# Time mixing with receptance and gate in plain fp32, and another order around the merges

## The chip, the cores and the metric

The kernel runs on one core of one Trainium2 chip. The metric is the device time of one execution in microseconds (us); of several executions the median counts. The engines are TensorE (PE in the profile, its weight loads PEld), VectorE (DVE), ScalarE (ACT), GpSimd (POOL) and SyncE (SP, whose queue issues the weight loads from HBM). A matmul writes one of eight PSUM banks of 128 x 512 fp32; everything else lies in SBUF.

## The reference, cut to what matters

Eight layers run one after the other on 256 tokens of width 1024. Only the first, a time mixing layer of the RWKV-7 kind, is touched:

```python
rkv = einsum('nbtd,nde->nbte', xs[:3], w_rkv)         # receptance r, key k, value v
w_log = -softplus(-(w0 + tanh(xw @ w1) @ w2)) - 0.5
a = sigmoid(a0 + (xa @ a1) @ a2)
g = sigmoid(xg @ g1) @ g2                             # gate, 160 -> 1024
# per head, token by token:
S = S * w + (S a) b^T + v k^T ;  y = S r
out = ((groupnorm(y) * lnx_w + lnx_b + sum(r * k * r_k) * v) * g) @ w_o
```

The last sum, `sum(r * k * r_k)`, is called the bonus below.

## The kernel before, in words

**Products.** The inputs are fp32. Large weights come in units of 128 x 1024 through a `Feeder`: a load from HBM fills one of four raw buffers (`s_slot_79` to `s_slot_82`), ACT writes a rounded copy `hi` in the fp32r format (line 88) and DVE the rest `lo = raw - hi` (line 89) into one of four cut buffers, and the raw buffer is loaded again. A product is then three fp32r matmuls (`mm3`, lines 290 to 292). The plan of units is k, v, r of `a_w_rkv` (8 units each), then `a_w_o` (8 units). A matmul on plain fp32 operands needs no split, and the trace shows each as two instructions.

**The recurrence** is solved in two blocks b of 128 tokens and two halves H of eight heads. `rwkv_keys` turns keys (PE transposes, line 1702 for those in pairs, 1716 for others); `rwkv_strict` makes the masked scores SM (PE line 1848, DVE line 1850). `rwkv_base` inverts 16 x 16 triangles for all heads on DVE: first line 1747, 14 rounds of lines 1768 and 1769, last line 1774. `rwkv_merge` doubles the inverted blocks twice: PE 1791, DVE copy 1792, PE 1798, DVE 1800 and 1804, PE 1811, DVE copies 1818, PE 1824, DVE copies 1827. `rwkv_solve` makes further scores SN (1848), multiplies them with V (1863), and then goes to and fro: ACT copy 1876, PE 1879, DVE copy 1880, PE 1874. `rwkv_query` scales and turns the queries (DVE 1934, PE 1702) and makes the bonus: POOL 1937, DVE 1938 and 1940, POOL 1943 to 1947. `rwkv_gate` multiplies the gate, split by `gate_parts` (ACT 1911 and 1913, POOL 1912, DVE 1907, 1910, 1914), on lines 290 to 292 and 1925. Then the output product with `a_w_o` begins, again on lines 290 to 292, and the next layer (`ffn0`, lines 532 and 534).

**Order.** Functions are generators that `weave` steps in turn, and a scheduler then fixes, when the kernel is built, one order of instructions for each engine and each queue from their dependences, the numbers given to `pri`, and its own notion of durations. On the chip each engine keeps its order: an instruction that waits holds all behind it, on the SP queue as well. PSUM banks are handed out in rings (`rings(acc, tp, long, po)`). In the listings `bank_67` to `bank_74` are the banks 0 to 7.

Of the kernel before, what the change touches and what calls it, by code (L numbers as in the profile page):

```python
# [29 lines left out]
class Feeder:  # L30
# [38 lines left out]
    def prime(self):  # L69
        k = self.k  # L70
        while self.n_dma < len(self.plan) and self.raw_free:
            shape, pieces = self.plan[self.n_dma]
            t = self.raw_free.pop(0)
            v = self.view(t, shape)
            for c0, c1, src in pieces:
                k.nc.sync.dma_start(v[:, :, c0:c1], src)
            self.raw[self.n_dma] = (t, v)
            self.n_dma += 1

    def _split(self):  # L80
        k, i = self.k, self.n_split
        self.prime()
        t, raw = self.raw.pop(i)
        cut = self.cut_free.pop(0)
# [8 lines left out]
        self.prime()  # L93

    def get(self):
# [53 lines left out]
class K:  # L149
# [148 lines left out]
    def gemm_b_steps(self, nkt, widths, lhs, done, rk=2, tail=0, head=0, before_b1=None):  # L298

        W = self.W  # L300
        for h, width in enumerate(widths):
# [3 lines left out]
            def mms(b, chunk, kt0, n):  # L305
                hi, lo, _ = chunk
                for i in range(n):
                    kt = kt0 + i
                    lh, ll = lhs(kt, b)
                    self.mm3(ps[b], lh, ll, hi[:, i, :], lo[:, i, :], kt == 0, kt == nkt - 1)  # L310
# [1060 lines left out]
    def plan_rwkv(self):  # L1371
        out = []
        for n in (1, 2, 0):
            out += plan_b(self.a["a_w_rkv"][0, n], D, D)
# [40 lines left out]
    def rwkv(self):  # L1415
# [151 lines left out]
        while len(self.bg) > 1:  # L1567
            self.tick()
        W.lo_pool = False
        gate = self.gate_parts(hid)  # L1570
        self.weave([self.pri(1000, self.rwkv_merge(E[H])) for H in range(2)] + [self.pri(400, self.rwkv_gate(H, E[H], *gate)) for H in range(0)], n=2)
        solve = ([self.pri(400, self.rwkv_solve(H, 0, E[H], raw["v"][H])) for H in range(2)]
                 + [self.pri(400, self.rwkv_gate(H, E[H], *gate)) for H in range(0, 2)])
        if 0:
            self.rings(2, 4, 2)
            self.weave(solve, n=0)
            solve = []
        self.drain()
        W.lo_pool = False
# [115 lines left out]
    def feat_pairs(self, src, out, zeroed=()):  # L1695

        nc = self.nc
        for b in range(2):
# [84 lines left out]
    def rwkv_merge(self, E):  # L1783
# [3 lines left out]
        p1 = self.tp()  # L1787
# [6 lines left out]
        pz = self.tp()  # L1794
# [11 lines left out]
        p1 = self.tp()  # L1806
# [13 lines left out]
        pz = self.tp()  # L1820
# [33 lines left out]

    def rwkv_solve(self, H, b, E, V):
# [3 lines left out]
        SN = yield from self.rwkv_scores(E, b, E["A2"][b], 1, 0)  # L1859
        pr = self.bank("long")  # L1860
        cols = [slice(hd * 64, hd * 64 + 64) for hd in range(8)]
        for hd, c in enumerate(cols):
            nc.tensor.matmul(pr[:, c], SN[:, hd], V[:, b, c], start=hd == 0, stop=False, skip_group_check=True)
# [33 lines left out]
    def gate_parts(self, hid):  # L1897

        nc, A = self.nc, self.a
        raw = [self.slot([128, D]) for _ in range(2)]  # L1900
        nc.sync.dma_start(raw[0], A["a_g2"][0, :128])
        for i in range(3):
            nc.sync.dma_start(raw[1][32 * i:32 * i + 32], A["a_g2"][0, 128:])
        gh, gl, gs = (self.slot([128, D], F32R) for _ in range(3))
        h = self.slot([128, 4, T], F32R)
        nc.scalar.activation(h[:, 0], hid[:, 2], AF.Copy)
        nc.vector.tensor_tensor(h[:, 1], hid[:, 2], h[:, 0], op=OP.subtract)
        for i in range(2):
            nc.scalar.activation(h[32 * i:32 * i + 32, 2], hid[:32, 3], AF.Copy)
        nc.vector.tensor_tensor(h[64:96, 2], hid[:32, 3], h[:32, 2], op=OP.subtract)  # L1910
        nc.scalar.activation(gh, raw[0], AF.Copy)
        nc.gpsimd.tensor_tensor(gl, raw[0], gh, op=OP.subtract)
        nc.scalar.activation(gs[:96], raw[1][:96], AF.Copy)
        nc.vector.tensor_tensor(gs[32:64], raw[1][32:64], gs[32:64], op=OP.subtract)
        return h, gh, gl, gs

    def rwkv_gate(self, H, E, h, gh, gl, gs):
# [11 lines left out]
    def rwkv_query(self, H, E, raw, vecs):  # L1929
# [4 lines left out]
        nc.vector.tensor_tensor(EP, R, EP, op=OP.mult)  # L1934
        E["R2"] = []
        yield from self.feat_pairs(EP, E["R2"])
# [134 lines left out]
```

## Time and profile before

| what | value |
|---|---|
| median of three executions | 1428.81 us (1420.3 to 1430.14) |
| the profiled execution | 1423.76 us, its span 1421.9 us |
| PE busy over the span | 1339.9 us (94%) |
| DVE, ACT, POOL busy | 982.4, 723.2, 312.1 us |
| layer of the change | from the start to some 300 us, where the next layer's matmuls are under way |

The span is the traced part of the profiled execution, 1.9 us less than its time. All times in the rows below count from the start of the span. Busy shares are means over eight layers with different limits; the part of the trace that the change touches lies between 60 and 300 us.

### The profile page before, as it was taken

The page shows a single profiled execution, that of the slowest core. Times are in us where ns is not written, and L with a number is a line of the kernel's source. Part 1 is how long each engine was busy: PE and PEld are TensorE (multiplying, and loading weights), DVE is VectorE, ACT ScalarE, POOL GpSimd, SP SyncE. Part 2 cuts the span into 40 slices and gives each one's busy share as a digit, 9 for nine tenths or more (in the row PEclk, how much of TensorE's full clock was granted, in tenths as well). Part 3 has the DMA queues.
Part 4 walks back from the last instruction along what each step waited for, and adds up shares of the span by engine and source line. Part 5 has one row for each costly group of instructions (what it writes and reads, how often), then busy time and mean ns, then how long its engine had stood idle before and what let it go on. Part 6 is the DMA issues. An engine that isn't in the chain of part 4 may idle for free. (4 is left out here: it accounts for less than half of the span.)

```text
span 1421.9 us, 20925 instructions
## 1 busy us (share of the span) xinstructions
PE 1339.9 (94%) x7819; PEld 1116.4 (79%) x7819; DVE 982.4 (69%) x1712; ACT 723.2 (51%) x1276; POOL 312.1 (22%) x278
## 2 busy tenths in 40 slices
PE   7998799989999799999999999999999998999998
PEld 5786699778888687788877777788888776788887
DVE  7889545788854675678864688677633897687642
ACT  5843212566643575576654555555543545465431
POOL 4201621100000100133222353222322631111110
PEclk9998599999999899999999999999999999999999
DMA  8345002466672452275574544265763632266662
GB/s 259 120 128 181 2 16 80 159 204 183 193 237 89 147 169 60 90 217 183 178 225 150 178 148 119 87 202 185 227 194 96 206 114 80 74 195 191 191 197 87
DMA packets 153574, 214.79 MB, mean 151 GB/s; under 512 B 11700, under 2 KB 95900, under 8 KB 153472
## 3 DMA queue, kind: packets, MB, share of 16 engines
q1 hardware_dynamic: 152608, 210.31, 47.6%
q10 hardware_dynamic: 864, 3.15, 0.6%
q8 instruction: 61, 1.00, 0.3%
q14 instruction: 41, 0.34, 0.1%
HBM read 212.37 MB, written 1.05 MB: 150 GB/s over the span
## 5 line engine op out<-in xcount | busy, mean ns | idle before, releaser
L88 ACT ACTIVATE s_slot<-s_slot 128x1024 fp32r<-128x1024 f32 (+2 forms) x221 | 229.6, 1045 | 166.8 <-PE bank L292 104.6
L89 DVE TENSOR_TENSOR s_slot<-s_slot,s_slot 128x1024 fp32r<-128x1024 f32 (+1 forms) x180 | 224.7, 1254 | 102.7 <-ACT s_slot L88 102.1
L89 DVE TENSOR_TENSOR rwkv_slot<-s_slot,rwkv_slot 128x1024 fp32r<-128x1024 f32 (+4 forms) x121 | 151.8, 1261 | 91.7 <-ACT rwkv_slot L88 91.2
L88 ACT ACTIVATE rwkv_slot<-s_slot 128x1024 fp32r<-128x1024 f32 (+3 forms) x141 | 144.7, 1034 | 88.3 <-PE bank L292 52.3
L89 POOL TENSOR_TENSOR s_slot<-s_slot,s_slot 128x1024 fp32r<-128x1024 f32 x41 | 100.9, 2460 | 303.0 <-ACT s_slot L88 283.0
L532 PE MATMUL bank<-ffn_slot,s_slot 128*128 128x512 f32 x320 | 115.2, 401 | 5.4 <-DVE ffn_slot L537 5.4
L532 PE MATMUL bank<-ffn_slot,rwkv_slot 128*128 128x512 f32 x280 | 98.4, 395 | 0.0
L532 PE MATMUL bank<-mlp_slot,s_slot 128*128 128x512 f32 x272 | 96.7, 396 | 0.6 <-DVE mlp_slot L537 0.6
L266 POOL TENSOR_TENSOR rwkv_sm<-rwkv_sm,mhalf 128x1 f32<-128x1 f32 x32 | 19.8, 618 | 340.0 <-DVE rwkv_sm L263 339.2
L534 PE MATMUL bank<-ffn_slot,s_slot 128*128 128x256 f32 x320 | 89.9, 281 | 0.0
L534 PE MATMUL bank<-ffn_slot,rwkv_slot 128*128 128x256 f32 x280 | 77.8, 278 | 0.0
L532 PEld LDWEIGHTS bank<-ffn_slot,s_slot 128*128 128x128 f32 x320 | 61.2, 191 | 20.8 <-DVE ffn_slot L537 6.4
L534 PE MATMUL bank<-mlp_slot,s_slot 128*128 128x256 f32 x272 | 75.8, 279 | 0.0
L89 POOL TENSOR_TENSOR rwkv_slot<-s_slot,rwkv_slot 128x1024 fp32r<-128x1024 f32 (+1 forms) x20 | 47.3, 2364 | 92.6 <-ACT rwkv_slot L88 75.1
L290 PE MATMUL bank<-s_slot,mlp_slot 128*128 128x512 f32 x160 | 62.6, 391 | 0.1
L292 PE MATMUL bank<-s_slot,mlp_slot 128*128 128x512 f32 x160 | 62.3, 390 | 0.0
L291 PE MATMUL bank<-s_slot,mlp_slot 128*128 128x512 f32 x160 | 62.3, 389 | 0.0
L532 PEld LDWEIGHTS bank<-ffn_slot,rwkv_slot 128*128 128x128 f32 x280 | 52.5, 188 | 12.4 <-DVE ffn_slot L537 0.3
L534 PEld LDWEIGHTS bank<-ffn_slot,s_slot 128*128 128x128 f32 x320 | 61.3, 192 | 0.0
L532 PEld LDWEIGHTS bank<-mlp_slot,s_slot 128*128 128x128 f32 x272 | 51.0, 188 | 12.8 <-DVE mlp_slot L537 0.9
L534 PEld LDWEIGHTS bank<-ffn_slot,rwkv_slot 128*128 128x128 f32 x280 | 52.6, 188 | 0.2
L532 PE MATMUL bank<-mlp_slot,rwkv_slot 128*128 128x512 f32 x144 | 51.7, 398 | 0.6 <-DVE mlp_slot L537 0.6
(514 smaller groups left out, 3549.4 us busy)
## 6 DMA issues: line engine op xcount, KB each, us to landing
s_slot<-in_mlp_w_dram SPq DMA_DIRECT2D x128, 512.0 KB, 4.4
s_slot<-in_ffn_w_in_dram SPq DMA_DIRECT2D x88, 512.0 KB, 4.2
s_slot<-in_ffn_w_out_dram SPq DMA_DIRECT2D x44, 512.0 KB, 4.2
s_slot<-in_a_w_rkv_dram SPq DMA_DIRECT2D x24, 512.0 KB, 4.4
s_slot<-in_diff_w_in_dram SPq DMA_DIRECT2D x32, 256.0 KB, 4.2
s_slot<-in_dsa_w_in_dram SPq DMA_DIRECT2D x16, 512.0 KB, 4.1
s_slot<-in_a_w_o_dram SPq DMA_DIRECT2D x8, 512.0 KB, 3.9
s_slot<-in_o_w_dram SPq DMA_DIRECT2D x8, 512.0 KB, 3.9
```

The costliest lines, as they stand in the source:

```text
L88: k.nc.scalar.activation(hi, raw, AF.Copy)
L89: (k.nc.gpsimd if low else k.nc.vector).tensor_tensor(lo, raw, hi, op=OP.subtract)
L266: nc.gpsimd.tensor_tensor(r, u, self.mhalf[:, 0:1], op=OP.pow)
L290: mm(out, lh, rh, start=start, stop=False)
L291: mm(out, lh, rl, start=False, stop=False)
L292: mm(out, ll, rh, start=False, stop=stop)
L532: mm(o, wh[:, kt % 4, c], a.rearrange("p c t -> p (c t)"), start=kt == 0, stop=False, skip_group_check=True)
L534: mm(o[:, :T], wl[:, kt % 4, c], a[:, 0], start=False, stop=kt == 7, skip_group_check=True)
```

## The change

Receptance units are marked whole in the plan: they are not split, `mm3` makes one plain fp32 matmul of them (line 307 of the changed kernel) from the unsplit token mix, and the raw buffer is given back when the matmuls have used it. The gate is one pair of plain fp32 matmuls (1943, 1944) on unsplit weights. `rwkv_solve_in` (scores SN of block 0 and their product with V) and the turn of the queries of block 0 are woven with the merges, the merges take their banks from a ring of their own, and the rest of `rwkv_query` is now `rwkv_bonus`, written behind the merges, with the loads of its vectors.

```diff
@@ Feeder._split
         t, raw = self.raw.pop(i)
+        if self.whole(i):
+            self.parts[i] = (raw, None, t)
+            self.n_split += 1
+            return
@@ Feeder.put
-        self._give(unit[2])
+        if unit[1] is None:
+            self.raw_free.append(unit[2])
+            self.prime()
+        else:
+            self._give(unit[2])
@@ Feeder.advance
-        while not self.hold and self.n_split < min(self.cap, len(self.plan)) and self.cut_free:
+        while not self.hold and self.n_split < min(self.cap, len(self.plan)) and (
+                self.cut_free or self.whole(self.n_split)):
+            self.prime()
+            if self.n_split not in self.raw:
+                return
             self._split()
@@ mm3
+        if rl is None:
+            mm(out, lh, rh, start=start, stop=stop)
+            return
@@ rwkv
-        xr = shifted(0, True)
-        self.bg.append(project("r", xr))
+        xr = shifted(0)
+        self.bg.append(project("r", (xr, xr)))
...
-        gate = self.gate_parts(hid)
-        self.weave([self.pri(1000, self.rwkv_merge(E[H])) for H in range(2)] + [...], n=2)
-        solve = ([self.pri(400, self.rwkv_solve(H, 0, E[H], raw["v"][H])) for H in range(2)]
-                 + [self.pri(400, self.rwkv_gate(H, E[H], *gate)) for H in range(0, 2)])
+        gate = self.gate_weights()
+        self.bg += [self.rwkv_gate(H, E[H], hid, gate) for H in range(2)]
         self.drain()
         W.cap = W.n_split
-        self.rings(0, 4, 4)
+        self.rings(0, 4, 2)
+        self.ring["merge"] = self.banks[6:]
+        self.weave([self.pri(1000, self.rwkv_merge(E[H])) for H in range(2)]
+                   + halves(400, self.rwkv_solve_in, raw) + halves(0, self.rwkv_query, raw, 0))
+        self.ring["long"] += self.ring["merge"]
         vecs = [...]
-        self.weave(solve + [self.pri(400, self.rwkv_query(H, E[H], raw, vecs)) for H in range(2)])
+        self.weave([self.pri(400, self.rwkv_solve(H, 0, E[H], raw["v"][H])) for H in range(2)]
+                   + [self.pri(0, self.rwkv_reads(E[H], 0)) for H in range(2)] + halves(0, self.rwkv_query, raw, 1)
+                   + halves(0, self.rwkv_bonus, raw, vecs))
@@ rwkv_gate
-            self.mm3(p, h[:, 0, t], h[:, 1, t], gh[:, cols], gl[:, cols], True, False)
-            nc.tensor.matmul(p, h[:96, 2, t], gs[:96, cols], start=False, stop=True)
+            nc.tensor.matmul(p, hid[:, 2, t], w[0][:, cols], start=True, stop=False)
+            nc.tensor.matmul(p, hid[:32, 3, t], w[1][:32, cols], start=False, stop=True)
```

What the scheduler makes of it shows in its orders. In the changed kernel the lines move on: 89 becomes 93, 290 to 292 become 309 to 311, 1702 is 1719, 1791 is 1808, 1792 is 1809, 1798 is 1815, 1850 is 1867, 1879 is 1911, 1880 is 1912, 1934 is 1950, 1937 is 1959, 1938 is 1960, 1940 is 1962.

VectorE before, from the end of the base (1774) to the first copies of the merges (1792):

```order
L1774 STREAM_TRANSPOSE rwkv_slot_796<-rwkv_slot_794 128x512
L1799 TENSOR_SCALAR rwkv_slot_1070<-rwkv_slot_796,even_odd 128x16x16 x2
L1850 TENSOR_TENSOR rwkv_slot_1508<-bank_67,rwkv_slot_97 128x512
L1938 TENSOR_TENSOR rwkv_slot_612<-rwkv_slot_503,rwkv_slot_612 128x1024
L1940 TENSOR_REDUCE rwkv_sm_496<-rwkv_slot_612 128x16
L1938 TENSOR_TENSOR rwkv_slot_613<-rwkv_slot_511,rwkv_slot_613 128x1024
L1850 TENSOR_TENSOR rwkv_slot_1512<-bank_68,rwkv_slot_97 128x512
L1792 COPY rwkv_slot_792<-bank_72 128x16x16
```

VectorE now, the same stretch (1791 is the end of the base, 1809 the first copy):

```order
L1791 STREAM_TRANSPOSE rwkv_slot_776<-rwkv_slot_774 128x512
L93 TENSOR_TENSOR s_slot_86<-s_slot_79,s_slot_85 128x1024
L1950 TENSOR_TENSOR rwkv_slot_511<-rwkv_slot_605,rwkv_slot_511 128x1024
L93 TENSOR_TENSOR s_slot_88<-s_slot_79,s_slot_87 128x1024
L1867 TENSOR_TENSOR rwkv_slot_1131<-bank_67,rwkv_slot_97 128x512
L1867 TENSOR_TENSOR rwkv_slot_1135<-bank_68,rwkv_slot_97 128x512
L1816 TENSOR_SCALAR rwkv_slot_982<-rwkv_slot_776,even_odd 128x16x16 x2
L93 TENSOR_TENSOR s_slot_90<-s_slot_79,s_slot_89 128x1024
L1722 COPY rwkv_slot_1140<-bank_69 64x4x128
L1722 COPY rwkv_slot_1150<-bank_70 64x4x128
L1960 TENSOR_TENSOR rwkv_slot_604<-rwkv_slot_503,rwkv_slot_604 128x1024
L1962 TENSOR_REDUCE rwkv_sm_496<-rwkv_slot_604 128x16
```

Behind these stand 1960 for the other half and then 1809: the bonus's instructions still stand ahead of the first merge copy, and three splits of `a_w_o` units (line 93), all from the raw buffer 79, and four evacuations came in ahead of it.

The SP queue before, from the first `a_w_o` unit on:

```order
L76 DMA s_slot_79<-in_a_w_o_dram 128x2x512
L76 DMA s_slot_80<-in_a_w_o_dram 128x2x512
L76 DMA s_slot_81<-in_a_w_o_dram 128x2x512
L76 DMA s_slot_82<-in_a_w_o_dram 128x2x512
L76 DMA s_slot_79<-in_a_w_o_dram 128x2x512
L76 DMA s_slot_80<-in_a_w_o_dram 128x2x512
L1901 DMA rwkv_slot_1071<-in_a_g_dram 128x1024
L1903 DMA rwkv_slot_1072<-in_a_g_dram 32x1024 x2
```

The SP queue now, from the same place (`in_a_g_dram` is the gate's weight, 248 the helper that loads a vector into all partitions):

```order
L76 DMA s_slot_79<-in_a_w_o_dram 128x2x512
L76 DMA s_slot_80<-in_a_w_o_dram 128x2x512
L76 DMA s_slot_79<-in_a_w_o_dram 128x2x512
L76 DMA s_slot_81<-in_a_w_o_dram 128x2x512
L1932 DMA rwkv_slot_983<-in_a_g_dram 128x1024
L1933 DMA rwkv_slot_984<-in_a_g_dram 32x1024
L76 DMA s_slot_79<-in_a_w_o_dram 128x2x512
L76 DMA s_slot_82<-in_a_w_o_dram 128x2x512
L76 DMA s_slot_79<-in_a_w_o_dram 128x2x512
L248 DMA rwkv_slot_1463<-in_a_r_k_dram 128x1024
```

The first four `a_w_o` units that are split now all pass through raw buffer 79, one after the other, since the other three are held by receptance units; the load of `a_r_k`, which the bonus needs, waits in the built program for the last gate matmul (1944), whose weight buffer it takes over.

TensorE now, from the end of the receptance (307) to the first merge matmuls (1808); before, lines 1848, 290 to 292 and 1925 of half 0 alone stood here:

```order
L307 MATMUL bank_68<-s_slot_82,rwkv_slot_595 128x512 x2
L1719 MATMUL bank_69<-ident,rwkv_slot_503 128x128 x4
L1865 MATMUL bank_67<-rwkv_slot_215,rwkv_slot_623 128x256 x2
L1865 MATMUL bank_68<-rwkv_slot_227,rwkv_slot_636 128x256 x2
L1943 MATMUL bank_72<-rwkv_slot_983,rwkv_slot_207 128x512
L1943 MATMUL bank_73<-rwkv_slot_983,rwkv_slot_207 128x512
L1943 MATMUL bank_74<-rwkv_slot_983,rwkv_slot_207 128x512
L1943 MATMUL bank_71<-rwkv_slot_983,rwkv_slot_207 128x512
L1944 MATMUL bank_72<-rwkv_slot_984,rwkv_slot_207 128x512
L1944 MATMUL bank_73<-rwkv_slot_984,rwkv_slot_207 128x512
L1944 MATMUL bank_74<-rwkv_slot_984,rwkv_slot_207 128x512
L1944 MATMUL bank_71<-rwkv_slot_984,rwkv_slot_207 128x512
```

All four gate products now stand ahead of the merges, and two scores of SN (1865) read banks that held the receptance.

## Rows read from the trace of the kernel before

**Rows 1.** Busy time by stretch: length, then PE, PEld, DVE, ACT, POOL; clock, DMA.

```profile
91.50:126.80 35.30, 34.37 (x282) 28.62 (x281) 29.69 (x53) 13.64 (x19) 1.56 (x3) 1.00 0.45 144
126.80:139.80 13.00, 6.14 (x17) 3.18 (x15) 12.29 (x20) 4.09 (x6) 2.35 (x1) 0.68 0.87 281
139.80:152.10 12.30, 5.95 (x264) 5.15 (x264) 10.48 (x12) 0.00 (x0) 8.42 (x5) 0.50 0.01 3
152.10:163.70 11.60, 7.74 (x385) 7.31 (x384) 4.06 (x7) 5.59 (x10) 11.17 (x8) 0.50 0.02 4
163.70:175.90 12.20, 12.12 (x150) 9.62 (x151) 7.06 (x11) 1.58 (x4) 3.39 (x7) 0.50 0.01 1
175.90:182.20 6.30, 6.30 (x47) 5.64 (x45) 1.50 (x3) 3.11 (x6) 4.83 (x3) 1.00 0.01 3
182.20:239.10 56.90, 56.82 (x521) 53.55 (x520) 28.30 (x54) 7.35 (x14) 9.39 (x31) 1.00 0.08 29
```

**Rows 2.** PE in order of time around the receptance: start, length, line, operands, count.

```profile
95.71 0.59 PE L290 MATMUL bank<-s_slot,rwkv_slot 128*128 128x512 f32 x1
...
124.06 0.39 PE L290 MATMUL bank<-s_slot,rwkv_slot 128*128 128x512 f32 x1
...
126.55 0.39 PE L292 MATMUL bank<-s_slot,rwkv_slot 128*128 128x512 f32 x1
126.78 2.28 PE L1848 MATMUL bank<-rwkv_slot,rwkv_slot 128*128 128x256 f32 x8
```

**Rows 3.** PE in order of time, plain fp32 matmuls at the full clock.

```profile
58.91 1.98 PE L1639 MATMUL bank<-rwkv_slot,rwkv_slot 128*128 128x512 f32 x4
60.82 1.91 PE L1526 MATMUL bank<-rwkv_slot,rwkv_slot 128*32 128x256 f32 x8
...
207.63 3.67 PE L1848 MATMUL bank<-rwkv_slot,rwkv_slot 128*128 128x256 f32 x16
211.13 0.78 PE L1963 MATMUL bank<-rwkv_slot,rwkv_slot 128*128 128x64 f32 x6
```

**Rows 4.** DVE groups from 105.4 to 141.1 us: count, busy, mean ns.

```profile
L89 DVE TENSOR_TENSOR s_slot<-s_slot,s_slot 128x1024 fp32r<-128x1024 f32 x7 | 8.5, 1218 | 0.3 <-ACT s_slot L88 0.2
```

**Rows 5.** DVE in order of time: base, bonus, first merge copies.

```profile
105.42 0.68 DVE L1747 TENSOR_TENSOR rwkv_slot<-bank,tri 128x512 f32<-128x512 f32 x1
...
131.41 2.10 DVE L1768 TENSOR_TENSOR rwkv_slot<-rwkv_slot 128x288 f32<-128x288 f32 x1
...
134.03 1.22 DVE L1914 TENSOR_TENSOR rwkv_slot<-rwkv_slot,rwkv_slot 32x1024 fp32r<-32x1024 f32 x1
...
140.32 0.71 DVE L1774 STREAM_TRANSPOSE rwkv_slot<-rwkv_slot 128x512 f32<-128x512 f32 x1
...
144.74 3.35 DVE L1938 TENSOR_TENSOR rwkv_slot<-rwkv_slot,rwkv_slot 128x1024 f32<-128x1024 f32 x1 [1.71 <-POOL rwkv_slot L1937]
148.12 1.22 DVE L1940 TENSOR_REDUCE rwkv_sm<-rwkv_slot 128x16 f32<-128x1024 f32 x1
...
150.99 0.75 DVE L1792 COPY rwkv_slot<-bank 128x256 f32<-128x256 f32 x2
```

**Rows 6.** Loads issued between 100 and 136 us: count, size, median us to landing.

```profile
s_slot<-in_a_w_o_dram SPq DMA_DIRECT2D x8, 512.0 KB, 3.9
...
rwkv_slot<-in_a_lnx_w_dram SPq DMA_DIRECT2D x1, 512.0 KB, 6.3
```

**Rows 7.** ACT and POOL in order of time: a split's first half, the bonus's products.

```profile
127.78 1.05 ACT L88 ACTIVATE s_slot<-s_slot 128x1024 fp32r<-128x1024 f32 x1
...
142.36 4.64 POOL L1937 TENSOR_TENSOR rwkv_slot<-rwkv_slot,rwkv_slot 128x1024 f32<-128x1024 f32 x2
```

**Rows 8.** PE in order of time: merges and the start of the solve.

```profile
139.85 2.85 PE L1791 MATMUL bank<-rwkv_slot,rwkv_slot 32*32 32x16 f32 x194 [3.34 <-DVE rwkv_slot L1772]
...
152.18 2.77 PE L1798 MATMUL bank<-rwkv_slot,rwkv_slot 32*32 32x16 f32 x186
156.07 1.25 PE L1798 MATMUL bank<-rwkv_slot,rwkv_slot 32*32 32x16 f32 x70 [1.13 <-issue]
159.14 3.65 PE L1811 MATMUL bank<-rwkv_slot,rwkv_slot 32*32 32x32 f32 x128 [1.82 <-DVE rwkv_slot L1804]
163.78 2.08 PE L1848 MATMUL bank<-rwkv_slot,rwkv_slot 128*128 128x256 f32 x4 [0.99 <-ACT rwkv_slot L1926]
...
182.23 2.07 PE L1879 MATMUL bank<-rwkv_slot,rwkv_slot 64*64 64x64 f32 x32
```

**Rows 9.** PE in order of time: where the output product waits.

```profile
252.11 0.50 PE L290 MATMUL bank<-s_slot,rwkv_slot 128*128 128x512 f32 x1 [0.89 <-ACT rwkv_slot L280]
```

More of the change, by code (lines that the diff above doesn't have):

```diff
@@ L93, in _split, with whole @@
         self.prime()
+    def whole(self, i):
+        return len(self.plan[i]) > 2
     def get(self):
@@ L1373, in plan_rwkv @@
         for n in (1, 2, 0):
-            out += plan_b(self.a["a_w_rkv"][0, n], D, D)
+            units = plan_b(self.a["a_w_rkv"][0, n], D, D)
+            out += units if n else [(*u, True) for u in units]
         return out + self.plan_out(self.a["a_w_o"][0], 4)
@@ L1693, in pair_tile, with feat_pairs @@
         return t
-    def feat_pairs(self, src, out, zeroed=()):
+    def feat_pairs(self, src, out, zeroed=(), bs=range(2)):
         nc = self.nc
-        for b in range(2):
+        for b in bs:
             t = zeroed.pop(0) if zeroed else self.pair_tile()
@@ L1786, in rwkv_merge @@
         Moff, P1z, Xv, Yc, Y32, Y64 = (E[n] for n in ("Moff", "P1z", "Xv", "Yc", "Y32", "Y64"))
-        p1 = self.tp()
+        p1 = self.bank("merge")
         for h in range(16):
@@ L1793, in rwkv_merge @@
         yield
-        pz = self.tp()
+        pz = self.bank("merge")
         for h in range(16):
@@ L1805, in rwkv_merge @@
         yield
-        p1 = self.tp()
+        p1 = self.bank("merge")
         for h in range(16):
@@ L1819, in rwkv_merge @@
         yield
-        pz = self.tp()
+        pz = self.bank("merge")
         for h in range(16):
@@ L1853, in rwkv_scores, with rwkv_known, rwkv_solve_in @@
         return S
+    def rwkv_known(self, E, b, V):
+        pr = self.bank("long")
+        for hd in range(8):
+            c = slice(hd * 64, hd * 64 + 64)
+            self.nc.tensor.matmul(pr[:, c], E["SN", b][:, hd], V[:, b, c], start=hd == 0, stop=False,
+                                  skip_group_check=True)
+        return pr
+    def rwkv_solve_in(self, H, E, raw):
+        E["SN", 0] = yield from self.rwkv_scores(E, 0, E["A2"][0], 1, 0)
+        E["pr"] = self.rwkv_known(E, 0, raw["v"][H])
+        yield
     def rwkv_solve(self, H, b, E, V):
@@ L1858, in rwkv_solve @@
         SM, Y = E["SM", b], E["Y64"]
-        SN = yield from self.rwkv_scores(E, b, E["A2"][b], 1, 0)
-        pr = self.bank("long")
         cols = [slice(hd * 64, hd * 64 + 64) for hd in range(8)]
-        for hd, c in enumerate(cols):
-            nc.tensor.matmul(pr[:, c], SN[:, hd], V[:, b, c], start=hd == 0, stop=False, skip_group_check=True)
+        if b:
+            E["SN", b] = yield from self.rwkv_scores(E, b, E["A2"][b], 1, 0)
+            pr = self.rwkv_known(E, b, V)
+        else:
+            pr = E["pr"]
         if b:
@@ L1895, in rwkv_solve, with gate_weights, rwkv_gate @@
                                         op=OP.mult)
-    def gate_parts(self, hid):
+    def gate_weights(self):
         nc, A = self.nc, self.a
[L1900 to L1917, printed above, removed]
+        w = [self.slot([128, D]) for _ in range(2)]
+        nc.sync.dma_start(w[0], A["a_g2"][0, :128])
+        nc.sync.dma_start(w[1][:32], A["a_g2"][0, 128:])
+        return w
+    def rwkv_gate(self, H, E, hid, w):
         nc = self.nc
@@ L1923, in rwkv_gate, with rwkv_query, rwkv_bonus @@
             t = slice(b * 128, (b + 1) * 128)
-            self.mm3(p, h[:, 0, t], h[:, 1, t], gh[:, cols], gl[:, cols], True, False)
-            nc.tensor.matmul(p, h[:96, 2, t], gs[:96, cols], start=False, stop=True)
+            nc.tensor.matmul(p, hid[:, 2, t], w[0][:, cols], start=True, stop=False)
+            nc.tensor.matmul(p, hid[:32, 3, t], w[1][:32, cols], start=False, stop=True)
             nc.scalar.activation(G[:, b], p, AF.Copy)
             yield
-    def rwkv_query(self, H, E, raw, vecs):
+    def rwkv_query(self, H, E, raw, b):
+        if b == 0:
+            self.nc.vector.tensor_tensor(E["EP"], raw["r"][H], E["EP"], op=OP.mult)
+            E["R2"] = []
+        yield from self.feat_pairs(E["EP"], E["R2"], (), (b,))
+    def rwkv_bonus(self, H, E, raw, vecs):
         nc = self.nc
```

17 lines of the change are left out of this document (3 added, 14 removed).

## Prediction

> **What bounds the kernel now.** I read the table of the span by slices first, then busy time by stretch in the layer of the change. There TensorE is the bound on both sides of a hole: it is busy for 34.37 of 35.30 us before 126.8 us and for 56.82 of 56.90 us behind 182.2 us, at a granted clock of 1.00 [rows 1]. Between them lie five stretches, 55.4 us in all, in which PE is busy for 38.25 us, most of that at a clock of 0.50 to 0.68. At 0.50, 1.2 GHz, the work takes twice as long as at 2.4 GHz: what stands there would take some 29.5 us without a gap at the full clock (the busy times of the rows, each times its clock: 4.2 + 3.0 + 3.9 + 6.1 + 6.3, is 23.5, and the small merge matmuls, paced by their issue, are not halved with the clock, which I put at 6 us more). So the hole loses some 25 us, and an edit gains only by shortening it or by taking dense PE work away.
>
> What holds the hole open is VectorE: the base runs there from 105.42 to 141.03 us, with seven splits (1.22 us each, 8.5 us) between its rounds [rows 4, 5]. Behind the base, the first merge matmuls are done soon after 139.85 [rows 8], but the first merge copy starts only at 150.99: two bonus multiplications and their sums stand ahead of it, and these wait for POOL's products of 4.64 us for the two halves [rows 5, 7]. Then the merges run back and forth between the engines, and the solve begins at 182.23.
>
> **The change, part by part.**
>
> *Receptance in plain fp32.* Before, a product is three instructions. They start 0.227 us apart: 32 products, 96 instructions, 21.8 us; they lie between 95.71 and 126.78, with masked scores in between [rows 2]. A plain fp32 matmul of 512 columns is two instructions: four took 1.91 us, 0.478 each, and 16 of 256 columns took 3.50 us, 0.219 each or 0.438 for 512 [rows 3]. So a product costs 0.88 to 0.96, and I take 0.90: 32 x 0.90 = 28.8 us. This is **+7.0 us** (6.3 to 8.8) on an engine that is dense there. With 0.9 us of idle time [rows 1] filled, the receptance ends at 126.8 + 7.0 - 0.9 = 133.
>
> *Gate in plain fp32.* Before, 16 instructions x 0.227 = 3.6 us. Now, eight matmuls, 16 instructions x 0.45 = 7.2 us, **+3.6 us** at the full clock. All of them now stand ahead of the merges.
>
> *VectorE's base.* In it, seven splits of 1.22 us become one, and the gate's splits go (some 2 us, one of them the 1.22 at 134.03), one query turn of 1.2 too, and the stretching of the 2.10 us round, beside POOL's gate split, from some 0.45 us [rows 4, 5]. That is 7.3 + 2 + 1.2 + 1.65 = 12.2 us of 35.6. The base gets its scores some 4 us sooner, as they stand ahead of the receptance. With waits for PE and ACT that I put at 6 to 7 us (the edits that gave them cover are gone), it ends at some 131 to 132, **9 to 10 us sooner** than 141.03. That is the gain which the merges could have.
>
> *What stands ahead of the merges now.* First, the `a_w_o` splits. The four that the order takes ahead of the copies all go through raw buffer 79, since the other three hold receptance. A round is a load of 3.9 us [rows 6], the first half of the split on ACT, 1.05 [rows 7], and the rest on DVE, 1.22 [rows 4]: with the hops 6.5 us. The buffer comes free when the fifth receptance unit is used, at 104.2 + 5 x 3.6 = 122. Rounds end at 128.5, 135, 141.5 and 148, and DVE holds the merge copies behind the last. Second, the scores of block 0 and the gate on PE: the scores wait for copies on ACT that stand behind one of those splits, 133 + 3.3 = 136.3, then the gate, to 143.5. The first merge matmuls end at 144 to 148 (before they started at 139.85). Third, the bonus: the load of `a_r_k` takes the gate's buffer, so it is issued at 143.5 and lands 3.9 to 6.3 us later [rows 6], at 147.4 to 149.8. Then POOL's first product of some 2.35 us, the multiplication beside POOL's second at 3.35, its sum 1.22 and the other multiplication 1.22 [rows 5, 7]: 147.4 + 8.1 = 155.5, or 157.9. The first merge copy therefore starts at **155.5 to 158**, against 150.99: +4.5 to +7. The base's gain is spent before the merges can use it; the bonus decides, with the chain of `a_w_o` splits close behind.
>
> *From the first copy to the solve.* Before, 182.23 - 150.99 = 31.2 us. The same chain of matmuls and copies remains, less the scores that moved ahead, with 24 scores and 8 turns of queries inside: the first pass 5.1, the scores behind it 3.6 (clock 1.00) to 7.6 (0.50), the second pass 3.65 [rows 8] twice, and between and behind them scores and turns of 3 to 4.8 and of 3.5 to 8.3. Added up, 18.9 to 33, of which I take 27, since in the rows before PE came back to 1.00 only behind 12 us of dense work at 0.50 [rows 1]. The solve then starts at some 156.8 + 27 = **183.8**, +1.6. A floor lies below it: the solve's first copies on DVE stand behind a masked score that waits for a PSUM bank and for the last of the bonus on POOL, which by the row at 142.36 and the pace after it is not done before 178.5; with 2.6 us for what lies between, 181.
>
> The Trainium skill, "TensorE: Matmul & The Clock Gate", section "Why this matters for your kernels", advises to keep TensorE busy without a break, and to leave no idle gaps between bursts of matmuls, to get its full clock. By that the scores woven with the merges would run at 1.00 at once, this sum would be some 22.3 instead of 27, and the floor of 181 would decide, for a time of some 1422. The trace speaks against it: PE was busy for 12.12 of 12.20 us from 163.7 on, and was still granted 0.50 [rows 1].
>
> *Behind the solve's start.* Ten score matmuls at 0.44 [rows 3] that stood at the full clock behind 182.2 are now done ahead: **-4.0 us** with their bank waits. The price is cover: the solve goes to and fro between PE, ACT and DVE, and less independent work stands between its steps: **+1**. And the output product, which waited for 0.89 us [rows 9], starts sooner than the work ahead of it on ACT and POOL does, which has not moved: **+2.5**, from 0 to 4. The loads of the next layer's weights keep their order.
>
> *Sum.* +1.6 - 4.0 + 1 + 2.5 = **+1.1 us** on the profiled execution's own 1423.76, so **1425**. That execution lies 5 us below the median of the three, 1428.81; 1425 is a difference of 0.3% from it. About 1%, 14 us, is what a measurement of this kernel tells from none.
>
> **Rivals.**
>
> *A, the hole closes.* The bonus and the splits don't hold the first copy: `a_r_k` and the buffers come early enough, DVE copies right behind the first matmuls, at 145 or 146, and the solve begins at 172 to 174. For it: VectorE really loses 12 us, and the base is the longest row of waits now. Against it: the bonus still stands ahead of the first copy in VectorE's order, and the floor from POOL's last product must go as well. It gives -8.5 to -10 in place of +1.6, so **1413** to 1415. Chance 0.15.
>
> *B, slower: one raw buffer.* The `a_w_o` rounds take the 6.3 us to land of the other 512 KB load [rows 6] rather than 3.9: four rounds, 4 x 2.4 = 9.6 us more. The last split ends at 157.6 rather than 148 and, as the bonus's multiplications stand behind it, the first copy at some 163; it decides from a round of some 8 us on, where the last split ends after `a_r_k`'s product. Beside it the receptance at its upper price (+1.8) and half the clock until the solve. For it: DMA is busy at 0.87 in the stretch from 126.8 [rows 1]. Against it: that traffic was these same eight loads at once, now strung out. It gives +10 to +15 on the sum, **1435** to 1440. Chance 0.2.
>
> *C, the clock stays at 0.50 until the solve.* The 27 become 32 to 33: +5, **1430**, which is within my main range. Chance 0.1.
>
> *D, the change doesn't do what it says.* The sums "behind the merges" are not behind the first merge copies in the orders, so this is already half the case, and in my sum. If only the rest of the reordering counts too, TensorE's +10.6 us would show undiminished, less the -4.0: 1430. Chance 0.05.
>
> **How the numbers follow.** The forecast has the other 0.5, 1418 to 1432 by its own ends (+1.6 from the floor's -1 to +7, output wait 0 to 4, price of the product -0.7 to +1.8). Range: down to A with the spread of 2 us that stands between the fastest executions and their mean, 1411, and up to B, 1441; 0.1 lies outside on either side. Within 1% of the median are 1414.5 to 1443: all of the forecast, C, D, most of B, and half of A. Against the median nothing that I can price reaches 1443 but B with a second loss; against an execution that happens to be slow in both, the bound moves. So faster 0.12, same 0.77, slower 0.11.
>
> **What would show it.** Receptance: two instructions a product, 0.43 to 0.48 each, ending at 132 to 134. Base: last transpose at 131 to 132. Rounds of 6 to 7 us on buffer 79. The gate ends at 143 to 144, `a_r_k` lands 4 to 6 us behind it, and the first merge copy starts at 155 to 158 behind the bonus's second multiplication. Granted clock 0.50 over the merges and 1.00 before the solve starts, at 181 to 186. The next layer's first matmuls at the same time as before, within 3 us. I am wrong if the first copy starts ahead of 150 (then A), behind 161 (B), or if the output product waits for more than 5 us.

## The result, and the profile after

The changed kernel takes **1436.94 us**, the median of seven executions (1435.14 to 1439.94); the kernel before takes 1427.14 us, also of seven (1417.63 to 1430.14). The ratio is 1.0088, with a 95% interval of 1.0066 to 1.0110: slower by 0.9%, or 9.8 us. The forecast was 1425, no change. The profiled execution took 1438.59 us with a span of 1436.5, 14.6 us more than the span of before.

From the page of the changed kernel, the span, the busy time of TensorE, and the clock by slices of 36 us:

```profile
span 1436.5 us, 20808 instructions
PE 1363.7 (95%) x7787; PEld 1127.5 (78%) x7787; DVE 969.3 (67%) x1699; ACT 709.7 (49%) x1261; POOL 307.7 (21%) x277
PEclk9999795999999899999999999999999999999999
```

The seventh slice, 215 to 251 us, is the one to see: a 5, in a place where the kernel before was at the full clock. Busy time by stretch shows it closer, with the columns of [rows 1]:

```profile
126.80:139.80 13.00, 12.36 (x37) 6.00 (x35) 6.19 (x8) 4.28 (x6) 3.01 (x6) 0.94 0.65 225
139.80:152.10 12.30, 9.40 (x274) 8.29 (x273) 8.94 (x8) 2.98 (x5) 6.39 (x3) 0.51 0.52 177
152.10:163.70 11.60, 9.40 (x285) 8.89 (x285) 4.86 (x8) 4.89 (x8) 11.52 (x7) 0.64 0.01 3
163.70:175.60 11.90, 11.90 (x291) 10.01 (x289) 8.62 (x14) 2.27 (x5) 11.69 (x31) 0.92 0.02 4
175.60:217.00 41.40, 39.88 (x375) 37.45 (x375) 22.00 (x48) 5.58 (x10) 4.25 (x10) 1.00 0.12 39
217.00:254.60 37.60, 37.60 (x166) 34.49 (x164) 11.35 (x15) 6.65 (x9) 2.12 (x3) 0.50 0.21 71
254.60:273.10 18.50, 17.84 (x86) 14.46 (x85) 14.04 (x27) 9.14 (x19) 3.97 (x3) 1.00 0.30 88
```

Two things happened. The hole ahead of the solve shrank: from 126.8 us to the solve's start there were 55.4 us with 17.2 us of idle TensorE, most at 0.50 [rows 1]; now there are 48.8 us with 5.7 us idle, and the clock comes back in between. The solve starts at 175.58 instead of 182.23, 6.65 us sooner. And a new loss opened behind it: from 217.0 to 254.6 us TensorE is busy without a gap, 37.60 of 37.60 us, at a granted clock of 0.50. At 1.00 the same work is taken to need half the time, so this costs some 18.8 us. The first product of the next layer starts at 273.12, against 265.08 before: +8.0 at the end of the layer. The other 6.6 us of the profiled spans arise in later layers, 2.3 of them by half clock, and were not followed; the medians differ by 9.8 in all.

Counted from the start of the span to the next layer, the difference of +8.0 is -11.6 us of idle TensorE (29.2 to 17.5 us), +6.8 us of half clock (47.8 to 61.4 us of it, half of the difference), and what is left, +12.9 us, which is put down to work. The plain products make +10.5 of that (28.4 for 21.8 us, 7.5 for 3.6); the other 2.4 were not followed.

What stands ahead of the fall is seen on TensorE and ScalarE, in order of time. TensorE (1898 finishes what the first solve copies of block 1 read, 1988 is the last part of block 0's output, 1911 and 1906 are solve steps of block 1):

```profile
196.79 3.74 PE L1898 MATMUL bank<-rwkv_slot,rwkv_slot 128*128 128x64 f32 x32
...
209.65 0.78 PE L1988 MATMUL bank<-rwkv_slot,rwkv_slot 128*128 128x64 f32 x6
210.26 1.08 PE L1865 MATMUL bank<-rwkv_slot,rwkv_slot 128*128 128x256 f32 x4
212.21 2.08 PE L1911 MATMUL bank<-rwkv_slot,rwkv_slot 64*64 64x64 f32 x32 [0.86 <-ACT rwkv_slot L1908]
214.94 2.06 PE L1906 MATMUL bank<-rwkv_slot,rwkv_slot 64*64 64x64 f32 x31 [0.66 <-DVE rwkv_slot L1912]
```

ScalarE in the same place (1999 are the squares of block 0's output, 1908 the solve copies):

```profile
210.60 0.60 ACT L1999 ACTIVATE rwkv_slot<-bank 128x512 f32<-128x512 f32 x1 [25.65 <-PE bank L1988]
...
211.09 0.59 ACT L1999 ACTIVATE rwkv_slot<-bank 128x512 f32<-128x512 f32 x1
...
211.57 1.07 ACT L1908 ACTIVATE rwkv_slot<-bank 64x512 f32<-64x512 f32 x2
```

The copies could have run from 200.4, when 1898 was done. They stand behind the squares in ScalarE's order, and these wait for 1988. In those 11 us TensorE uses up the scores that could have covered the solve; then it waits for the copies, 0.86 us, and for DVE, 0.66 us. Before, the copies (then 1876) stood ahead of the squares (then 1977): ScalarE ran them at 207.65 and the squares at 228.09:

```profile
207.65 1.07 ACT L1876 ACTIVATE rwkv_slot<-bank 64x512 f32<-64x512 f32 x2 [14.38 <-PE bank L1866]
...
228.09 0.60 ACT L1977 ACTIVATE rwkv_slot<-bank 128x512 f32<-128x512 f32 x1 [7.13 <-PE bank L1966]
```

ScalarE's orders say so without a run: eight copies and then the squares before; four copies, block 0's two squares and then the other four copies now.

### The profile page after: what moved, and what is told of

Same layout as the page of the kernel before. It is cut to its first block, busy times and chain, and to the rows that moved or that the text cites. A ratio compares the mean times of both kernels' runs of the same rounds, so it can differ in the third digit from the quotient of the medians.

```text
span 1436.5 us, 20808 instructions
## 1 busy us (share of the span) xinstructions
PE 1363.7 (95%) x7787; PEld 1127.5 (78%) x7787; DVE 969.3 (67%) x1699; ACT 709.7 (49%) x1261; POOL 307.7 (21%) x277
## 3 DMA queue, kind: packets, MB, share of 16 engines
q1 hardware_dynamic: 152512, 210.04, 47.1%
## 5 line engine op out<-in xcount | busy, mean ns | idle before, releaser
L92 ACT ACTIVATE s_slot<-s_slot 128x1024 fp32r<-128x1024 f32 (+2 forms) x213 | 220.9, 1044 | 162.3 <-PE bank L311 84.4
L93 DVE TENSOR_TENSOR s_slot<-s_slot,s_slot 128x1024 fp32r<-128x1024 f32 (+3 forms) x172 | 215.5, 1259 | 107.6 <-ACT s_slot L92 107.4
```

## The experiments

**Theory 1, the wait:** the reordering lets the output of block 0 start early, its squares hold the solve copies of block 1 on ScalarE, TensorE runs dry there, and its clock falls. **Theory 2, the price:** the loss is the plain fp32 products, some 10 us more of TensorE, which is also what the medians differ by. Half clock "in the solve" means from the solve's start to the first product of the next layer, in the profiled execution; the kernel before has none there. Ratios are to the kernel before on the same chip, whose median was 1422.9 to 1425.4 in the four groups of runs. Every execution, profiled or not, has its span and mean granted clock on record: below, span times clock is called its work, and the rest of the span the clock's loss. For the change the medians are 1386.0 us of work and 50.3 of loss; for the kernel before, in the four groups, 1383.0 to 1384.0 and 37.0 to 39.8.

**copy_first.** The change with one edge of order, the squares behind the solve copies:

```diff
+            first = nc.scalar.activation(Rs[s], pr[s], AF.Copy)      # rwkv_solve
+            if b and not i:
+                self.first.append(first.ins)
...
+        while len(self.first) < 2:
+            yield
+        with self.tc.issue_after(self.first[0]), self.tc.issue_after(self.first[1]):
             nc.scalar.activation(sq, py, AF.Square, scale=0.125)     # rwkv_out
```

> The changed kernel, with ScalarE's squares of block 0's output (line 1999) ordered behind the first two solve copies of block 1 (line 1908). Theory 1, the wait: the loss is half the clock over 37.6 us in block 1's solve and the output product, after TensorE stood idle for 0.86 and 0.66 us behind those squares; then these gaps and the half-clock stretch go, and the time falls by 15 to 19 us, to 1418 to 1422. Theory 2, the price: the loss is the plain fp32 products, 6.5 us of receptance and 3.9 of gate on TensorE; then the order of two copies moves the time by under 3 us, 1434 to 1439.

1425.3 us (ten executions, 1418.0 to 1430.6), ratio 1.0007 (0.9980 to 1.0033): 11.6 us under the change, and level with before. Theory 2 falls by this: no product has changed. Theory 1 named 1418 to 1422, which only the shorter executions reach. Its ScalarE, and TensorE by stretch:

```profile
201.33 1.07 ACT L1908 ACTIVATE rwkv_slot<-bank 64x512 f32<-64x512 f32 x2 [15.47 <-PE bank L1898]
...
216.36 0.60 ACT L2004 ACTIVATE rwkv_slot<-bank 128x512 f32<-128x512 f32 x1 [1.80 <-PE bank L1990]
...
176.50:217.00 40.50, 40.50 (x382) 38.01 (x382) 17.62 (x41) 5.74 (x11) 0.88 (x25) 1.00 0.05 14
217.00:254.60 37.60, 36.50 (x222) 32.56 (x221) 25.84 (x43) 14.12 (x23) 10.69 (x10) 0.91 0.32 105
```

The copies run at 201.33, TensorE is busy for 40.50 of 40.50 us, and of the 37.6 us at 0.50 there are 6.8 left. The next layer starts at 259.1, 14.0 us sooner than in the change. Over all executions the work is the same, 1385.8 us for 1386.0, and the clock's loss is 37.7 for 50.3. The edge moves TensorE's order too: scores (1865) stand between block 1's solve steps again.

**reads_late.** The query scores of block 0 back where they were:

```diff
-                   + [self.pri(0, self.rwkv_reads(E[H], 0)) for H in range(2)] + halves(0, self.rwkv_query, raw, 1)
+                   + halves(0, self.rwkv_query, raw, 1)
```

> The changed kernel, with the score products of block 0's queries (rwkv_reads of block 0) made in rwkv_out again, as before, and not woven with block 0's solve; this undoes one part of the reordering. Theory 1: those scores are cover for block 1's solve again and ScalarE's copies stand ahead of the squares, so the half clock there goes: 1418 to 1424. Theory 2: 1434 to 1439.

1446.9 us (four executions), ratio 1.0175 (1.0137 to 1.0213): slower than the change, against both theories. Its copies do stand ahead of the squares. But block 0's solve now has nothing beside it, and the first steps wait; by stretch, and from the waits of TensorE from 170 to 285 us:

```profile
183.00:203.60 20.60, 20.12 (x132) 18.86 (x133) 6.34 (x11) 1.08 (x2) 0.00 (x0) 0.51 0.01 2
...
240.00:257.60 17.60, 17.60 (x80) 16.92 (x81) 10.08 (x13) 4.98 (x6) 4.09 (x4) 0.52 0.25 84
...
PE bank L1911 <- DVE rwkv_slot L1844: 3.8, 1, 3.8
```

That points to cover as the scarce thing: once the scores SN of block 0 have gone to the merges, those of the queries are needed in block 0's solve. Theory 1 needs this addition: not the copies' order alone, but what work is left beside each solve.

**r_plain** and **g_plain.** The kernel before, with one of the products plain:

```diff
 r_plain
+            out += units if n else [(*u, True) for u in units]      # and Feeder, mm3, xr as in the change
 g_plain
+        gate = self.gate_weights()                                  # and rwkv_gate as in the change
```

> The kernel before, with receptance alone in plain fp32. Theory 2: plus 6.5 us, 1433 to 1436. Theory 1: the products cost 6.5 us ahead of 127 us, but VectorE's base ends sooner, and the hole up to the solve takes back 2 to 6 of it; the solve's order stays as before and the clock at 1.00 there: 1427 to 1432.

> The kernel before, with the gate alone in plain fp32 (no split of its weight or input). Theory 2, the price: 3.9 us more on TensorE at the full clock, 7.8 at half: 1429 to 1433. Theory 1: the gate stands inside the hole, where TensorE has room, and the splits it saves stand ahead of the merges: 1421 to 1427.

r_plain: 1419.7 us, ratio 0.9994 (0.9969 to 1.0019). g_plain: 1426.6, ratio 1.0043 (1.0017 to 1.0069). Theory 2 wanted 1433 and 1429 at the least, with a kernel before at some 1427. For r_plain that fails by the ratio too, -4.4 to +2.7 us against +6.5. For g_plain it does not: +2.4 to +9.8 us holds the 3.9 to 7.8 that Theory 2 named. But its work is not longer, 1383.5 us for 1384.0; its clock's loss is 41.3 for 37.0. In r_plain the first merge copy starts at 138.87 instead of 150.99 and the solve at 174.19: the 6.6 us on TensorE buy more than that back in the hole.

**both_plain.** Both products plain, none of the reordering.

> The kernel before with receptance and gate in plain fp32 and nothing of the reordering. Theory 2, the price: 10 us more of TensorE, 1430 to 1436. Theory 1: the hole ahead of the solve takes both back, and the solve has its cover and its copies ahead of the squares as before: 1420 to 1428.

1419.2 us (twelve executions), ratio 0.9963 (0.9939 to 0.9987): a little *faster* than before, with all of the price in it. Theory 2 is refuted as the cause of the loss: the price shows in the work, 1388.2 us for 1383.5, and the clock's loss is 29.7 for 39.8. By stretch, up to the solve and through it:

```profile
126.00:172.00 46.00, 37.29 (x865) 26.67 (x864) 30.68 (x36) 13.94 (x22) 33.03 (x22) 0.81 0.35 117
172.00:260.00 88.00, 86.50 (x653) 76.04 (x652) 53.44 (x99) 24.53 (x47) 12.44 (x38) 1.00 0.25 79
```

**r_split.** The change with receptance split again: `out += units`, `xr = shifted(0, True)`.

> The changed kernel, with receptance split into fp32r parts again; gate and order as changed. The squares stay ahead of the solve copies in ScalarE's order. Theory 2: minus 6.5 us, 1430 to 1432. Theory 1: the half-clock stretch in the solve stays (30 us or more at 0.50 behind the solve's start), the receptance's 6.5 us come off and VectorE's splits, 8 x 1.22 us, come back in the base, so 1430 to 1440.

1425.1 us, ratio 1.0005 (0.9982 to 1.0027), 11.8 us under the change, more than either theory gave it. The half clock in the solve is 17.1 us there, not 30: the loss behind the squares (TensorE waits for 1908 for 1.7 us) is not the same size in each kernel.

**order_bare** and **order_only.** The reordering with every product split as before; order_only has the edge of copy_first too. Both differ from the change in `gate_parts` and `mm3` in `rwkv_gate`, taken from the kernel before, and the two lines of r_split.

> The reordering alone, with all products split as before, and ScalarE's squares of block 0 ahead of the solve copies of block 1, as the change has them. If the wait for these copies costs whatever the products are: 4 to 12 us over the same kernel with the copies first (1419), so 1423 to 1431. If the waits matter only beside plain products: 1418 to 1421.

> As the run before, and the gate split into fp32r parts again too: what is left of the change is the order alone (scores and query turns next to the merges, bonus, banks), with the squares behind the solve copies. If the price of the plain gate on TensorE counts ahead of the merges: 2 to 4 us under the run before, 1413 to 1418. If the gate's splits on VectorE, ScalarE and POOL hold the merges as they did in the kernel before: 0 to 8 us over it.

order_bare: 1433.95 us, ratio 1.0055 (1.0024 to 1.0086), above the 1423 to 1431 that was named. order_only: 1419.2, ratio 0.9963 (0.9942 to 0.9983). So the reordering alone loses, without a plain product in it, and the one edge turns its loss into a gain. In order_bare:

```profile
207.67 0.60 ACT L2012 ACTIVATE rwkv_slot<-bank 128x512 f32<-128x512 f32 x1 [0.44 <-PE bank L2001]
...
208.16 1.06 ACT L1908 ACTIVATE rwkv_slot<-bank 64x512 f32<-64x512 f32 x2
...
217.00:254.60 37.60, 37.60 (x160) 34.27 (x159) 10.99 (x14) 6.13 (x9) 3.01 (x4) 0.51 0.20 70
```

Squares (there 2012), then copies, then 41.0 us of half clock, behind waits of 1.16 and 1.90 us: the picture of the change. order_only has 13.7 us of half clock in the solve, and a clock's loss of 34.0 us for order_bare's 48.7, with the work within 0.7. order_only was named 2 to 4 us under split_first or up to 8 over; it is 1.8 under, within the intervals of both, and the gate's price there stays undecided.

**split_first.** r_split with the edge of copy_first.

> The changed kernel with receptance split into fp32r parts again and ScalarE's squares behind the solve copies of block 1; gate in plain fp32. If the wait of the copies cost that kernel 17 us of half clock in the solve (with receptance split, profiled: 1425), it goes, and layer one ends at some 253 us: 1416 to 1421. If the copies' order only helps where receptance is plain: 1424 to 1427.

1421.0 us, ratio 0.9979 (0.9958 to 0.9999), at the upper end of the first case. But the profile doesn't show what was expected: TensorE waits for no solve copy on ScalarE, and the clock falls all the same, for 17.1 us from 216.8, right behind one wait of 0.67 us for a solve copy on DVE; of TensorE from 196 to 234 us, the row that has a wait, and by stretch:

```profile
216.47 3.30 PE L1987 MATMUL bank<-rwkv_slot,rwkv_slot 128*128 128x64 f32 x16 [0.67 <-DVE rwkv_slot L1914]
...
216.80:233.90 17.10, 17.10 (x77) 16.59 (x77) 10.10 (x13) 4.87 (x6) 3.49 (x3) 0.50 0.25 80
```

With 3.4 us more of it near the solve's start, that is 20.5 us of half clock where r_split had 17.1: in these two profiles the edge gained no clock in the solve.

**fill.** The change with eight matmuls of 128x512 on the squares and the scaled output of block 0, results unread, so that TensorE has work where it waited; on ScalarE the squares still stand ahead of the copies:

```diff
+    def fill(self, rhs):
+        p = self.tp()
+        for _ in range(2):
+            self.nc.tensor.matmul(p, self.ident, rhs, start=True, stop=True)
...
         nc.scalar.activation(sq, py, AF.Square, scale=0.125)            # rwkv_out
+        if not b:
+            self.fill(sq)
         nc.vector.tensor_tensor(yc, py, E["G"][:, b], op=OP.mult)
+        if not b:
+            self.fill(yc)
```

> The changed kernel with eight matmuls of 128x512 more (each two instructions, some 0.9 us, whose results nobody reads) on block 0's squares and scaled output, which stand on TensorE ahead of and between the solve steps of block 1 where it stood idle for 0.86 and 0.66 us. ScalarE's order is as changed, so the wait itself stays. If the half clock in the solve (37.6 us) comes from those idle gaps: it goes or falls under 10 us, and 7 us of more work less 1.5 us of gaps less 14 to 19 us give 1423 to 1429. If it comes from the kind of work behind (64x64 and 64-column matmuls), the half clock stays and the time rises by 4 to 7 us, 1441 to 1444.

1427.3 us, ratio 1.0035 (1.0008 to 1.0062), 9.7 us under the change (7.6 by the ratios) with more work in it. No half clock is left in the solve:

```profile
177.70:217.00 39.30, 39.30 (x339) 35.13 (x339) 17.99 (x41) 5.10 (x9) 3.81 (x4) 1.00 0.04 14
217.00:254.60 37.60, 37.33 (x258) 31.30 (x258) 22.12 (x33) 11.34 (x20) 4.62 (x5) 1.00 0.30 100
```

But more than the gaps was changed. The scheduler put block 0's output ahead of 1898, which the copies read, so that the squares hold them no longer; ScalarE:

```profile
205.53 1.08 ACT L2004 ACTIVATE rwkv_slot<-bank 128x512 f32<-128x512 f32 x2 [18.43 <-PE bank L1993]
...
208.38 0.59 ACT L1908 ACTIVATE rwkv_slot<-bank 64x512 f32<-64x512 f32 x1 [1.29 <-PE bank L1898]
```

And scores (1865) stand between the solve steps again, beside the new matmuls. So the same solve steps and output product run at 1.00 here, where TensorE has no gap ahead of them and other work between them; which of the two did it, this run doesn't say, and that "the wait itself stays" did not hold.

**merge_first** and **both_first.** The bonus's DVE instructions (1960, 1962) behind the first merge copies (1809), in the change and in copy_first:

```diff
+        with self.tc.issue_after(self.merged[0]), self.tc.issue_after(self.merged[1]):   # the two copies
             nc.vector.tensor_tensor(R, EP, R, op=OP.mult)
             nc.vector.tensor_reduce(bon, heads(R), axis=AX.X, op=OP.add)
```

> The changed kernel with the bonus's first DVE instructions (1960, 1962) behind the first merge copies (1809). As the prediction has it, the bonus decides when the first copy starts: it goes from 151.5 to some 148 us and the solve's start from 175.6 to 172; the half clock in the solve stays: 1432 to 1436. If the bonus doesn't decide: solve within 1 us of 175.6, 1436 to 1439.

> The changed kernel with both orders: the bonus's DVE instructions behind the first merge copies, and ScalarE's squares behind the solve copies of block 1. If the two losses are apart, it is the 1425 of the kernel with the squares moved, less 2 to 4 us: 1421 to 1424, with the solve starting at some 173.

merge_first: 1435.3 us (1423.9 to 1445.0), ratio 1.0097 (1.0057 to 1.0138). both_first: 1428.5, ratio 1.0041 (1.0019 to 1.0063). Neither gains, and both_first misses the 1421 to 1424 that was named. merge_first's profiled execution, one of its shorter, starts the solve at 180.05, at half clock over 30.7 us of the merges. In its solve TensorE has the order of the change, and waits in the same two places:

```profile
216.59 2.08 PE L1911 MATMUL bank<-rwkv_slot,rwkv_slot 64*64 64x64 f32 x32 [0.77 <-ACT rwkv_slot L1908]
219.32 2.02 PE L1906 MATMUL bank<-rwkv_slot,rwkv_slot 64*64 64x64 f32 x31 [0.66 <-DVE rwkv_slot L1912]
...
217.00:254.60 37.60, 36.69 (x263) 32.53 (x262) 21.25 (x32) 9.73 (x17) 8.70 (x9) 0.86 0.26 95
```

The clock falls behind them as in the change, but for 10.2 us and not 37.6; with the edge, in both_first, it falls for 17.1. So the two waits have no fixed price. In both_first the first copy comes 5.4 us sooner than in copy_first, and the solve 0.6 us sooner (175.86 for 176.49):

```profile
147.75 0.76 DVE L1809 COPY rwkv_slot<-bank 128x256 f32<-128x256 f32 x2 [3.49 <-PE bank L1808]
...
153.06 1.99 PE L1815 MATMUL bank<-rwkv_slot,rwkv_slot 32*32 32x16 f32 x189
...
175.86 2.07 PE L1913 MATMUL bank<-rwkv_slot,rwkv_slot 64*64 64x64 f32 x32
```

Between the copy and the next merge pass, TensorE has 5.3 us of known products and scores to do, most of it at half the clock. The bonus stands beside them, all but off the path; of the 4.8 us that were gained at the copy and not at the solve, 3.4 us more of half clock ahead of the solve than in copy_first make 1.7.

## Why the prediction was wrong

**Right: the parts ahead of the merges, in size.** Receptance 28.8 us, measured 28.4; gate 7.2, measured 7.5; a round through raw buffer 79 6.5, measured 6.2; `a_r_k` landing 3.9 to 6.3 us behind the gate, measured 4.2; the first merge copy 12 us behind the gate's end, measured 12.4:

```profile
L307 PE MATMUL bank<-s_slot,rwkv_slot 128*128 128x512 f32 x64 | 28.4, 592 | 0.0
...
131.51 3.60 PE L1943 MATMUL bank<-rwkv_slot,rwkv_slot 128*128 128x512 f32 x8
135.03 4.02 PE L1944 MATMUL bank<-rwkv_slot,rwkv_slot 32*128 32x512 f32 x8
138.98 1.12 PE L1719 MATMUL bank<-ident,rwkv_slot 128*128 128x128 f32 x4
...
139.08 0.35 SPq L248 DMA_DIRECT2D rwkv_slot<-in_a_r_k_dram  x1
...
143.30 4.65 POOL L1959 TENSOR_TENSOR rwkv_slot<-rwkv_slot,rwkv_slot 128x1024 f32<-128x1024 f32 x2 [12.55 <-DMA rwkv_slot<-in_a_r_k_dram]
...
151.45 0.76 DVE L1809 COPY rwkv_slot<-bank 128x256 f32<-128x256 f32 x2
```

**Off: when that stretch begins.** Receptance was to end at 133 and the gate at 143.5; they end at 128.6 and 139.0, because ten receptance matmuls already run from 90.97 us on, among the value products. The first copy is at 151.45 and not at 155.5 to 158. The base ended at 127.5 and not at 131 to 132, because it began at 98.06, 7.4 us sooner and not 4; its length, 29.5 us, is what the sum gave (35.6 less 12.2, and 6.5 of waits). It doesn't matter, since nothing waited for it.

**Wrong: that the bonus, by way of the first copy, sets the solve's start.** The first copy does start right behind the bonus, at 151.45, but both_first moves the bonus away and the solve stays within 0.6 us. In the changed order TensorE has its own work between the passes, and that is the path. The kernel before had less of it there, 7.74 of 11.60 us from 152.1 on [rows 1], and the argument was carried over from it.

**Wrong: the clock up to the solve.** 27 us from the first copy to the solve were put down on the ground that it comes back only behind 12 us of dense work; it took 24.1. (The sum's low end, 18.9, counts the second pass of 3.65 once where the text says twice; by its own terms it is 22.5. The ends of the forecast add up to 1419 and 1434, not 1418 and 1432. Neither bears on the miss.) The clock came back for a while in the middle and again from some 166 us on. With the two points before it the solve starts at 175.58 (forecast 183.8): **-6.65 and not +1.6.** The Trainium skill, "TensorE: Matmul & The Clock Gate", section "Why this matters for your kernels", advises to leave no idle gaps between bursts of matmuls. By that the prediction had 22.3 us in place of 27, and the 24.1 lie between the two: the dense stretch from 163.70 on has a mean clock of 0.92, where 0.50 stood in [rows 1], but the stretches ahead of it have 0.51 and 0.64.

**The step that failed: "The price is cover: [...] less independent work stands between its steps: +1".** The mechanism is named there, and its price is not 1 us but 18.8 us of half clock with 1.5 us of waits ahead of it. The waits are about what was estimated; what was missing is that TensorE's clock fell behind them. Half of the evidence lay open: ScalarE's orders, where squares and copies change places (every place in the orders that the prediction rests on lies ahead of the solve). That waits this short could be followed by a fall, no row of before showed: in [rows 1] the clock falls in a stretch with 6.9 us of idle time in 13.0, and it stays at 1.00 behind the 0.89 us of [rows 9]. From the solve's start to the next layer there were 82.85 us before and there are 97.54 now: +18.8 of clock, +1.2 of waits, and what is left, -5.3 of work, which the forecast had at -4.0 for the scores. The +2.5 ahead of the output product did not come; it waits 0.45 us, before 0.89 [rows 9]. With -6.65 for the hole these make the +8.0 of the layer. So two errors stand against each other, 8.3 us too long up to the solve and 15.2 too short behind it; that the forecast of the layer, +1.1, is only 6.9 us off is in part luck. Of the three signs that would have shown it wrong (first copy ahead of 150 or behind 161, the output product's wait above 5 us) none came: none of them looks at the solve.

**The rivals.** A was near with the solve's start, 172 to 174, but not with its way there: the first copy was to start at 145 or 146. B did not come: the rounds took 6.2 us, and its time, 1435 to 1440, was met for another reason. What D says of the orders is true, the bonus stands ahead of the first copy, and it cost nothing. Rival C put the clock's loss in the merges, not in the solve.

**What stays open.** That the order of squares and copies makes the loss, through the clock and not through more work, is shown by one edge in two pairs of kernels, the first two here; two more point the same way. Medians over all executions:

| pair, without and with the edge | ratio to before | clock's loss, us | work, us |
|---|---|---|---|
| the change, copy_first | 1.0088, 1.0007 | 50.3, 37.7 | 1386.0, 1385.8 |
| order_bare, order_only | 1.0055, 0.9963 | 48.7, 34.0 | 1382.6, 1383.3 |
| r_split, split_first | 1.0005, 0.9979 | 39.9, 34.8 | 1383.0, 1383.9 |
| merge_first, both_first | 1.0097, 1.0041 | 47.1, 41.4 | 1385.0, 1385.0 |

In the last two pairs the intervals of the ratios overlap, and the profiled executions, one of each, don't show the gain in the solve: 17.1 and 20.5 us of half clock, 10.2 and 17.1. Five profiled kernels have no half clock in the solve: before, r_plain, g_plain, both_plain and fill; the first four have the old order there.

What of the new order takes the clock is not separated. The falls in block 1's solve come behind waits, but their length doesn't follow them: 37.6 us behind 0.86 and 0.66, 10.2 behind 0.77 and 0.66, 41.0 behind 1.16 and 1.90, 17.1 behind 1.69 (r_split) and behind 0.67, and behind 0.83 once 17.1 (both_first) and once 6.8 (copy_first). And in before, r_plain, g_plain and both_plain TensorE waits for 0.89 us ahead of 128x512 products, and the clock stays at 1.00. The rival to the waits is the work: with the change's order the solve steps of block 1 stand one behind the other with no scores between them, and both copy_first and fill, which bring the scores back, close these gaps at the same time. A run with the gaps and the scores, or with neither, is missing.

## What to carry to other kernels

When a change moves work from one place to another as filler, ask what it filled before: here the hole ahead of the solve got shorter by 6.65 us, partly by scores that had stood between the solve's steps, and the solve with less between them paid some 18.8 in clock. Compare the orders of every engine to the end of the layer, ScalarE's too; a consumer that becomes ready early can stand in front of the step on the path, and one edge of order (here worth 0.8% of the kernel) puts it back. Don't price a short wait on a dense TensorE by its length alone: waits of 0.67 to 1.90 us were followed here by 6.8 to 41.0 us of half clock, and others of 0.89 by none. When times of one kernel spread, split each into work and clock's loss before comparing. The parts that gained here are both_plain and order_only, each at 0.9963 of the kernel before.

## What the runs showed of the hardware that was not expected

Being busy, as the profile counts it, was not enough for the clock to come back: from 217.0 to 254.6 us TensorE was busy for 37.60 of 37.60 us at 0.50, in a mix of 128x64 matmuls and fp32r products which in the kernel before, and in fill, ran at 1.00 throughout. It rose to 1.00 at some 254.3, after the output product's 128x512 matmuls had run alone from 250.5 on. In merge_first it rose at 232.0, inside the same mix.

Executions of one kernel differ by their clock: for the kernel before, in one group of 25, the times go from 1417.0 to 1428.5 us with clocks from 0.978 to 0.968. The work is 1386.0 us for the change and 1383.0 for that group (medians of 7 and 25 executions), 0.2% apart, while their mean clocks, 0.965 and 0.972, are 0.7% apart. The plain products' work nearly vanishes in the first (it fills what was idle), and most of the slowdown is in the second. fill has the most work, 1392.0, with a clock of 0.976, and is faster than the change.
